# One encoder layer on one core: the convolution of a pair in two blocks, more first operands before the last norm, the last norm's steps together, the third block of output weights earlier

## The chip, the cores and the metric

The kernel runs on one core of a Trainium2 chip. The metric is the device time of one execution in microseconds (us); lower is better. A core has five engines that run their own instruction lists in order and wait for each other through semaphores: TensorE (PE in the profile), VectorE (DVE), ScalarE (ACT), GpSimd (POOL) and SyncE (SP, which here issues transfers). PE writes its sums to eight banks of PSUM; DVE and ACT read them from there. The projections keep fp32 accuracy with three matmuls over a high and a low part of each operand.

## The reference

One layer of an encoder over 1024 positions of width 1024. Only the second half matters for this change:

```
hn = rms_norm(x, norm1_g);  proj = hn @ w_in
out_a = global_gqa_attention(...);  out_b = dilated_mixture_attention(...)
mixed = concat([rms_norm(out_a, outa_norm_g), rms_norm(out_b, outb_norm_g)])
x = x + mixed @ w_out
h = rms_norm(x, norm2_g)
u = h @ w_up                                   # 1024 x 5632
u = conv(u, conv_w, width 3, per channel) + conv_b
x = x + (gelu(u[:, :2816]) * u[:, 2816:]) @ w_down
```

## The kernel before

**Stages.** The profiled execution shows them one after the other on PE: the first projection, mixer A (attention), mixer B (dilated windows), the output projection `mixed @ w_out` with the second norm (to about 683 us), the up projection with convolution and gate (683 to 1085 us), and the down projection (to the end at 1330 us).

**The output projection and the last norm.** It goes over eight row blocks i of 128 positions. `h2_a(i)` adds the residual on DVE (L929), takes the squares on ACT (L935), and forms the norm's factor in a chain of one-element operations on DVE and one square root on ACT (L936, L937, L938, the four steps of a Newton iteration at L191 to L194); L942 writes the normed rows `hn(i)`. `h2_b(i, half)` transposes these on PE (L180, four per half) and takes the result out of PSUM into the operands of the up projection: L204 and L957 to L965, with sums and differences of row blocks that the seven-product scheme below needs. `t_split` (L972 on ACT, L973 on DVE) splits such a sum into high and low part. The last two blocks are 6 and 7. PE does the first two products of the up projection while norm 7 is made, then the transposes of block 7.

**The up projection.** It takes the channels in 22 pairs j of two channel tiles (u = 0, 1). Even pairs hold gate channels, the odd pair behind them the matching value channels. A pair is computed by a fast scheme with seven products of half size instead of eight; `product` (L1247 to L1249) is twelve matmuls. The products of a pair come in the order n = 1, 6, 7, 5, 2, 4, 3. The seven results are put together by copies on ACT (n = 1 and 2, L1254 and L1264) and by adds on DVE (L1251, for n = 6, 7, 5, 4 and 3). Four PSUM banks serve the even pairs and four the odd ones. Within a pair n = 4 writes the bank of n = 7, and n = 3 that of n = 5, so PE can start n = 4 only when DVE has done the add of n = 7, and n = 3 only after the add of n = 5.

`wu_prep(m)` makes the first operand of a product some products ahead: sums of weight blocks on POOL (L1221, L1222, L1224, L1226), the high part on ACT (L1230), the low part on DVE, or on POOL for n = 2 and 4 (both L1231). `conv(j, u)` is the convolution of a channel tile: the middle tap with the bias on ACT (L1278, 1024 positions), then four side taps on DVE (L1280: two of 768 positions and two of 255). `gate(j, u)` is the gelu on ACT (L1284) and the product on DVE (L1285) for two pairs together, and `gate_sums` the sums that the down projection needs, on POOL (L1294, behind one-element operations L1299), with stores to a scratch in HBM.

**What sets the order.** The functions are called in a written order, and a scheduler fixes each engine's list from it before the run. Where the author wants an order that the data do not force, a copy of one element (a "tick") writes into a place that a later operation overwrites, after reading something that must be done first. In the loop over products, the convolutions of both tiles of pair j are called right behind its product n = 3, and, for an odd pair, the two gates behind them. On DVE that puts eight taps and two gate products in one run between the add of n = 3 and the adds of the next pair.

**Weights of the output projection.** `wo_load` and `wo_split` bring its eight blocks of weights in and split them (L869 on ACT, L874 on DVE), some during mixer A and some between the heads of mixer B.

Of the kernel before, what the change touches and what calls it, by code (L numbers as in the profile page):

```python
# [14 lines left out]
AF = mybir.ActivationFunctionType  # L15
# [4 lines left out]
D = 1024  # L20
# [83 lines left out]
R_T4 = R_W + 4096  # L104
R_OP = [R_W + 8192, R_W + 9216, R_K2A + 6144, R_K2A + 7168, R_K2A + 4096, R_K2A + 5120]
# [18 lines left out]
def tile_encoder_layer(ctx, tc, x, w_in, gains, outg, norm1_g, norm2_g, w_out, w_up, conv_w, conv_b,  # L124
# [84 lines left out]
    def qab(tt):  # L209
        return O_QAB + 1024 * tt  # L210
# [493 lines left out]
    def load_tmx(h):  # L704
        dma(f(F_TMX[h % 2], 1344), tmx[h])
# [181 lines left out]
    def mix_t(i):  # L887
        return SM_T + 16 * (i % 3)
# [36 lines left out]
    def h2_a(i):  # L925
        t = SM_T + 48 + 8 * (i % 2)
        o = qab(seq(i))
        for hf in range(2):
            vec.scalar_tensor_tensor(f(o + 512 * hf, 512), bank(pj(i, hf)), f(mix_t(i) + 6, 1),  # L929
                                     f(F_X + 1024 * (i % 2) + 512 * hf, 512), op0=OP.mult, op1=OP.add)  # L930
        if i < 6:
            act(f(hn(i), 1024), f(o, 1024), AF.Square, accum_out=f(t, 1))
        else:
            for hf in range(2):
                act(f(hn(i) + 512 * hf, 512), f(o + 512 * hf, 512), AF.Square, accum_out=f(t + 5 + hf, 1))  # L935
            vec.tensor_tensor(f(t, 1), f(t + 5, 1), f(t + 6, 1), op=OP.add)  # L936
        vec.tensor_scalar(f(t + 1, 1), f(t, 1), 1.0 / D, EPS, op0=OP.mult, op1=OP.add)  # L937
        act(f(t + 2, 1), f(t + 1, 1), AF.Sqrt)  # L938
        newton(f(t + 3, 1), f(t + 1, 1), f(t + 2, 1), f(t + 4, 1))
        n = 1024 if i < 6 else 512  # L940
        for k in range(0, 1024, n):
            vec.scalar_tensor_tensor(f(hn(i) + k, n), f(o + k, n), f(t + 3, 1), f(F_G2 + k, n), op0=OP.mult, op1=OP.mult)  # L942
        dma(rscr[seq(i)], f(o, 1024))
# [3 lines left out]
    def h2_b(i, half):  # L947
        b = next_tr()
        for k in range(4):
            tr_f(b, k, f(hn(i) + 512 * half + 128 * k, 128))  # L950
        pair, x0 = seq(i) % 4, xs(i)
        t1, t2, t3, t4 = [t_raw(n, pair) for n in (1, 2, 3, 4)]
        if seq(i) < 4:
            evac_split(x0 + 512 * half, b)
            act((t1, t4)[half], bank(b), AF.Copy)
        elif half == 0:
            act(t3, bank(b), AF.Copy)  # L957
            vec.tensor_tensor(t1, bank(b), t1, op=OP.subtract)
            act(r(x0, 512), t1, AF.Copy)
            (gp if i < 6 else vec).tensor_tensor(r(x0 + 1024, 512), t1, rf(x0, 512), op=OP.subtract)  # L960
        else:
            evac_split(x0 + 512, b)
            vec.tensor_tensor(t2, bank(b), t1, op=OP.subtract)
            vec.tensor_tensor(t3, bank(b), t3, op=OP.subtract)
            (gp if i < 6 else vec).tensor_tensor(t4, t4, t2, op=OP.subtract)  # L965

    def t_raw(n, i):
        return f((F_TA[i], qab(i + 4) + 512, qab(i + 4), F_TD[i])[n - 1], 512)

    def t_split(n, i, eng):  # L970
        o = (R_T2, R_T3, R_T4)[n - 2] + 1024 * i
        act(r(o, 512), t_raw(n, i), AF.Copy)  # L972
        eng.tensor_tensor(r(o + 512, 512), t_raw(n, i), rf(o, 512), op=OP.subtract)  # L973

# [139 lines left out]
    for g in range(16):  # L1114

        prep += a_prep(g + 1) if g < 15 else []
        if g == 14:
            prep += [lambda: b_split(0)] + b_prep(0)
        tail = a_main(g, prep, tail, late, {14: (1, 1, 1, 1, 1, 2, 2, 2), 15: (2, 2, 2, 2, 1, 1, 1, 1)}.get(
            g, (1, 1, 1, 1, 1, 1, 1, 0)),  # L1120
                      (0, 2, 2, 2, 1, 1, 1, 1))
        if g == 7:
            dma(f(F_CNT, 384), cnt)
            gp.memset(fp(F_VCN + 64, [66, 8]), 1.0)
            load_vc(0)
        if g in (4, 7):
            wo_load(g // 7)
        if g == 9:
            load_tmx(1)
# [143 lines left out]
    def conv(j, u):  # L1273
        c = tile_of(j, u)
        i = F_U[2 * (j % 2) + u]
        a = acc(j, u)
        w = [f(O_CW + 44 * t + c, 1) for t in range(4)]
        act(f(a, 1024), f(i, 1024), AF.Identity, scale=w[1], bias=w[3])  # L1278
        for w_, o, d, n in ((w[0], 256, 0, 768), (w[0], 1, 768, 255), (w[2], 0, 256, 768), (w[2], 768, 1, 255)):
            vec.scalar_tensor_tensor(f(a + o, n), f(i + d, n), w_, f(a + o, n), op0=OP.mult, op1=OP.add)  # L1280

    def gate(j, u):
        a, v = acc(j - 1, u), acc(j, u)
# [136 lines left out]
    for i in range(8):  # L1420
        if i < 7:
            proj_out(i + 1, 0, 0)
            mix_tr(i + 1, 1)
            proj_out(i + 1, 0, 1)
        if i == 6:
            wu_load(1)
            for m in range(4):
                wu_prep(m)
            for q in range(2):
                t_split(2, q, vec)  # L1430
        if 0 < i < 7:
# [12 lines left out]
        if i < 6:  # L1444
            x_load(i + 2)
# [6 lines left out]
    h2_b(7, 0)  # L1452
    h2_b(7, 1)
    t_split(2, 3, vec)
    for o in (F_S[0], F_S[2]):

        vec.tensor_copy(f(o, 1), f(mix_t(7) + 10, 1))
    wu_prep(4)
    for q in range(4):
        t_split(3, q, vec)  # L1460
    wu_prep(5)
    for q in range(4):
        t_split(4, q, vec)
    dealt = []
    for m in range(2, len(order)):
        j, n = order[m]
        product(m)
        wu_prep(m + 4)

        if n in (2, 4) or n == 3 and j % 2 == 0 or n == 1 and j % 2:  # L1470
            take(dealt, 1)
        if n == 3 and j < NPAIR - 1:
            conv(j, 0)
            conv(j, 1)
            if j % 2:
                gate(j, 0)
                gate(j, 1)
                dealt += gate_sums(j)
        if j == NPAIR - 1:
            if n == 5:  # L1480
                for q in range(4):
                    d_load(q)
            if n == 4:
                d_prep(0)
                d_load(4)
            if n == 3:
                d_prep(1)
                d_prep(2)
                d_load(5)
                d_load(6)  # L1490
    last = NPAIR - 1
    for m in range(len(steps)):
        n, q = steps[m]
        down(m)
        d_prep(m + 3)
        if m < 2:
            conv(last, m)
# [68 lines left out]
```

## Time and profile before

| | |
|---|---|
| median of three runs | 1331.51 us (1330.01 to 1332.91) |
| the profiled execution, its own time | 1332.38 us |
| its span | 1330.6 us |
| PE busy | 1301.8 us (98%) |
| DVE busy | 1013.6 us (76%) |
| ACT busy | 681.6 us (51%) |
| POOL busy | 387.0 us (29%) |

PE's busy time is near the span, so a gain can only come from the few places where PE stands or runs at a lower clock, and a loss from new ones. The shares of the other engines are means over the whole span; in the up projection DVE is far above its mean. An engine's idle time is printed with what ended it, in brackets: `[0.58 <-DVE bigf L1251]` means that the engine stood for 0.58 us and went on when DVE's instruction of line 1251 was done.

### The profile page before, as it was taken

How to read it: one execution, taken by the hardware profiler on the slowest of the kernel's cores; microseconds unless marked ns; L12 is line 12 of the kernel's file. 1: busy time of each engine (PE TensorE's matmuls, PEld its weight loads, DVE VectorE, ACT ScalarE, POOL GpSimd, SP SyncE). 2: the span in 40 equal slices, each digit the busy share in tenths (PEclk: the TensorE clock that was granted, in tenths of full speed). 3: DMA queues.
4: the chain of work that ended last, by engine and by line, in shares of the span. 5: the costliest groups of instructions: out<-in, count | busy, mean ns of one | idle time of the engine just before them, and what ended most of it. 6: DMA issues, size and time to landing. Idle time of an engine off the chain costs nothing.

```text
span 1330.6 us, 20124 instructions
## 1 busy us (share of the span) xinstructions
PE 1301.8 (98%) x7559; PEld 1130.2 (85%) x7559; DVE 1013.6 (76%) x1599; ACT 681.6 (51%) x1070; POOL 387.0 (29%) x304
## 2 busy tenths in 40 slices
PE   7999999999999999999999999999999999999998
PEld 7999999999999888878877888888888888888887
DVE  4987687556655777876588999999999999586664
ACT  7855564555545676674365344444444445244341
POOL 0611122000111222100115666556756653100000
PEclk9999999999999999999999999999999999999999
DMA  7145211001002454443122322322232325897873
GB/s 258 52 112 127 80 40 52 17 1 36 2 9 61 99 143 114 99 144 111 64 88 72 119 103 103 103 89 95 103 119 101 106 95 190 303 309 231 295 229 105
DMA packets 120500, 152.28 MB, mean 114 GB/s; under 512 B 50962, under 2 KB 77010, under 8 KB 119890
## 3 DMA queue, kind: packets, MB, share of 16 engines
q1 hardware_dynamic: 118609, 143.65, 33.4%
q0 software_dynamic: 1792, 7.34, 2.5%
q8 instruction: 59, 0.97, 0.3%
q14 instruction: 40, 0.32, 0.1%
HBM read 112.95 MB, written 33.82 MB: 110 GB/s over the span
## 4 chain that ended last, share of the span: by engine, by line
PE 79%; DVE 12%; ACT 4%; issue 4%; DMA 1%; SPq 0%; DVEq 0%; ACTq 0%
PE ps L659 8%; PE ps L1247 7%; PE ps L1248 7%; PE ps L1249 7%; PE ps L1380 5%; PE ps L1378 5%; PE ps L1379 5%; DVE bigf L1280 5%; PE ps L411 4%; PE ps L412 3%; PE ps L413 3%; PE ps L664 3%; PE ps L637 2%; PE ps L665 2%; PE ps L918 2%
## 5 line engine op out<-in xcount | busy, mean ns | idle before, releaser
L1247 PE MATMUL ps<-bigr 128*128 128x512 f32 x616 | 241.8, 393 | 6.2 <-DVE bigf L1251 5.6
L1248 PE MATMUL ps<-bigr 128*128 128x512 f32 x616 | 240.3, 390 | 0.0
L1249 PE MATMUL ps<-bigr 128*128 128x512 f32 x616 | 240.1, 390 | 0.0
L1280 DVE SCALAR_TENSOR_TENSOR bigf<-bigf 128x768 f32<-128x768 f32 (+1 forms) x176 | 178.5, 1073 | 26.4 <-ACT bigf L1278 26.3
L1230 ACT ACTIVATE bigr<-bigf 128x512 fp32r<-128x512 f32 x154 | 93.2, 625 | 139.4 <-POOL bigf L1222 70.3
L659 PEld LDWEIGHTS ps<-bigf 128*128 128x128 f32 x1024 | 139.6, 191 | 10.4
L1247 PEld LDWEIGHTS ps<-bigr 128*128 128x128 f32 x616 | 116.1, 188 | 34.9 <-DVE bigf L1251 9.0
L1358 ACT ACTIVATE bigr<-bigf 128x1024 fp32r<-128x1024 f32 x77 | 80.8, 1060 | 118.8 <-PE ps L1380 85.7
L1249 PEld LDWEIGHTS ps<-bigr 128*128 128x128 f32 x616 | 116.0, 188 | 24.4
L1248 PEld LDWEIGHTS ps<-bigr 128*128 128x128 f32 x616 | 116.1, 188 | 23.6
L659 PE MATMUL ps<-bigf 128*128 128x65 f32 x1024 | 135.0, 267 | 0.0
L411 PE MATMUL ps<-bigr 128*128 128x256 f32 x448 | 127.2, 284 | 1.2 <-ACT bigf L295 1.2
L1231 DVE TENSOR_TENSOR bigr<-bigf,bigr 128x512 fp32r<-128x512 f32 x112 | 125.2, 1135 | 3.2 <-ACT bigr L1230 2.6
L412 PE MATMUL ps<-bigr 128*128 128x256 f32 x448 | 126.8, 283 | 0.0
L413 PE MATMUL ps<-bigr 128*128 128x256 f32 x448 | 126.7, 283 | 0.0
L667 ACT ACTIVATE bigf<-ps 128x512 f32<-128x512 f32 x128 | 76.0, 597 | 93.5 <-PE ps L665 92.4
L1378 PE MATMUL ps<-bigr 128*128 128x512 f32 x308 | 119.8, 389 | 0.0
L1380 PE MATMUL ps<-bigr 128*128 128x512 f32 x308 | 119.8, 389 | 0.0
L1379 PE MATMUL ps<-bigr 128*128 128x512 f32 x308 | 119.8, 389 | 0.0
L1359 DVE TENSOR_TENSOR bigr<-bigf,bigr 128x1024 fp32r<-128x1024 f32 x77 | 93.0, 1222 | 26.0 <-ACT bigr L1358 25.0
L638 DVE TENSOR_REDUCE bigf<-ps 128x1 f32<-128x512 f32 x128 | 86.3, 690 | 23.5 <-PE ps L637 21.6
L411 PEld LDWEIGHTS ps<-bigr 128*128 128x128 f32 x448 | 85.8, 192 | 1.9 <-ACT bigf L295 1.6
(233 smaller groups left out, 2870.0 us busy)
## 6 DMA issues: line engine op xcount, KB each, us to landing
bigf<-w_down SPq DMA_DIRECT2D x99, 256.0 KB, 4.3
bigf<-w_up SPq DMA_DIRECT2D x44, 512.0 KB, 3.6
bigf<-gscr SPq DMA_DIRECT2D x77, 256.0 KB, 4.0
gscr<-bigf SPq DMA_DIRECT2D x33, 512.0 KB, 2.6
bigf<-w_in SPq DMA_DIRECT2D x8, 1024.0 KB, 5.1
bigf<-x SPq DMA_DIRECT2D x15, 512.0 KB, 7.0
bigf<-tmx SPq DMA_DIRECT2D x8, 672.0 KB, 5.5
bigf<-w_out SPq DMA_DIRECT2D x8, 512.0 KB, 4.8
```

The source lines that it names most:

```text
L411: mm(o, ah, wh, start=(k == 0 and t % 2 == 0 and n != 2), stop=False, skip_group_check=True)
L412: mm(o, ah, wl, start=False, stop=False, skip_group_check=True)
L413: mm(o, al, wh, start=False, stop=(k == 3), skip_group_check=True)
L659: mm(bank(ob, 65, 66 * i), f(slots[kt] + 128 * i, 128), f(F_VA + 132 * kt + 66 * kv, 65), start=(kt == 0 and i == 0), stop=(kt == 7), skip ...
L1231: (gp if n in (2, 4) and m > 3 else vec).tensor_tensor(rp(o + 512, [128, 4], [1, 128]), src, rfp(o, [128, 4], [1, 128]), op=OP.subtract)
L1247: mm(bank(b), wh, th, start=(k == 0 and n in (1, 5, 6, 7)), stop=False, skip_group_check=True)
L1248: mm(bank(b), wh, tl, start=False, stop=False, skip_group_check=True)
L1249: mm(bank(b), wl, th, start=False, stop=(k == 3), skip_group_check=True)
L1280: vec.scalar_tensor_tensor(f(a + o, n), f(i + d, n), w_, f(a + o, n), op0=OP.mult, op1=OP.add)
L1378: mm(o, ah, r(d, 512), start=(q == 0 and n in (1, 5, 2)), stop=False, skip_group_check=True)
L1379: mm(o, ah, r(d + 1024, 512), start=False, stop=False, skip_group_check=True)
L1380: mm(o, al, r(d, 512), start=False, stop=(q == NQ - 1), skip_group_check=True)
```

## The change

There are four parts.

1. **The last norms' steps together.** For blocks 6 and 7 the mean and the constant are added to the first half's sum as soon as it is there, and one operation joins the second half; one step leaves the chain. A tick that reads `hn(7)` (L958 of the new code) now stands in front of the evacuations of block 6, and such a tick (L980) in front of the splits of T3 and T4 for two of their four parts, so that on DVE all this comes behind norm 7. Two subtractions of block 6 go from DVE to POOL.
2. **Two more first operands ahead.** `wu_prep(4)` and `wu_prep(5)` are called before the last norm with the first four; the places of six operand buffers and two weight blocks move for it.
3. **The convolution in two blocks.** `conv` now returns two blocks per tile: the middle tap with the two taps of `w[0]`, and the two taps of `w[2]`. The loop does one block behind each of the products n = 1, 6, 7 and 5 of the next pair. The middle tap of u = 1 waits for a tick (L1290) that reads what the add of the next pair's n = 7 writes. The two gates come one each behind n = 2 and n = 4 of the even pair, the four steps of the gate sums behind n = 3 of the even pair and n = 1, 6 and 7 of the odd one. Twenty-one ticks are added.
4. **The third block of output weights.** Block 4 is loaded and split during mixer A, instead of loaded behind mixer A and split in the last head of mixer B; the other loads and splits move one place.

```diff
-F_WOR = [O_F + o for o in (4960, 4960, 2560, 3616, 6304, 4960, 2560, 6304)]
+F_WOR = [O_F + o for o in (4960, 4960, 2560, 3616, 3616, 4960, 6304, 2560)]
...
-            vec.tensor_tensor(f(t, 1), f(t + 5, 1), f(t + 6, 1), op=OP.add)
-        vec.tensor_scalar(f(t + 1, 1), f(t, 1), 1.0 / D, EPS, op0=OP.mult, op1=OP.add)
+                if hf == 0:
+                    vec.tensor_scalar(f(t, 1), f(t + 5, 1), 1.0 / D, EPS, op0=OP.mult, op1=OP.add)
+            vec.scalar_tensor_tensor(f(t + 1, 1), f(t + 6, 1), 1.0 / D, f(t, 1), op0=OP.mult, op1=OP.add)
...
+        if i == 6:
+            vec.tensor_copy((r(x0 + 1536, 1), f(qab(seq(6) % 4 + 4), 1))[half == 0], f(hn(7), 1))
...
+        if n > 2 and i < 2:
+            vec.tensor_copy(r(o, 1), f(hn(7), 1))
...
-    for k, (g0, kt) in enumerate(((6, 4), (8, 4))):
+    for k, g0, kt in ((0, 6, 4), (4, 7, 4), (1, 8, 4)):
...
-    wo_early = {(5, 0): [(wo_load, 2)], (6, 0): [(wo_load, 3), (wo_load, 4)], (7, 0): [(wo_load, 5)],
-                (7, 1): [(wo_split, 2), (wo_load, 6)], (7, 3): [(wo_split, 3)], (7, 5): [(wo_split, 4), (wo_load, 7)]}
+    wo_early = {(5, 0): [(wo_load, 2)], (6, 0): [(wo_load, 3), (wo_load, 6)], (7, 0): [(wo_load, 5)],
+                (7, 4): [(wo_split, 3)], (7, 5): [(wo_split, 2), (wo_load, 7)]}
...
-        act(f(a, 1024), f(i, 1024), AF.Identity, scale=w[1], bias=w[3])
-        for w_, o, d, n in ((w[0], 256, 0, 768), (w[0], 1, 768, 255), (w[2], 0, 256, 768), (w[2], 768, 1, 255)):
-            vec.scalar_tensor_tensor(f(a + o, n), f(i + d, n), w_, f(a + o, n), op0=OP.mult, op1=OP.add)
+        def mid():
+            if u and j < last:
+                vec.tensor_copy(f(a, 1), f(F_U[2 * ((j + 1) % 2) + 1], 1))
+            act(f(a, 1024), f(i, 1024), AF.Identity, scale=w[1], bias=w[3])
+
+        def side(w_, *spans):
+            for o, d, n in spans:
+                vec.scalar_tensor_tensor(f(a + o, n), f(i + d, n), w_, f(a + o, n), op0=OP.mult, op1=OP.add)
+
+        return [lambda: (mid(), side(w[0], (256, 0, 768), (1, 768, 255))),
+                lambda: side(w[2], (0, 256, 768), (768, 1, 255))]
...
-            for m in range(4):
+            for m in range(6):
                 wu_prep(m)
...
-        if n in (2, 4) or n == 3 and j % 2 == 0 or n == 1 and j % 2:
-            take(dealt, 1)
-        if n == 3 and j < NPAIR - 1:
-            conv(j, 0)
-            conv(j, 1)
+        if n == 3 and j < last:
+            taps += conv(j, 0) + conv(j, 1)
             if j % 2:
-                gate(j, 0)
-                gate(j, 1)
+                gates += [lambda j=j, u=u: gate(j, u) for u in range(2)]
                 dealt += gate_sums(j)
+        else:
+            take(taps, 1)
+        if j % 2 == 0 and n in (2, 4):
+            take(gates, 1)
+        if n == 3 and j % 2 == 0 or n in (1, 6, 7) and j % 2:
+            take([] if gates else dealt, 1)
```

What the scheduler makes of it is read from the engines' lists. In the new code the lines from the up projection on are higher: the matmuls L1247 to L1249 are L1255 to L1257, the low part L1231 is L1239, the add L1251 is L1259, the taps L1280 are L1295, the gate L1285 is L1303, the gate sums L1294 and L1299 are L1312 and L1317, and the norm's last write L942 is L945.

DVE around the last norm. Before, from L937 to the write of `hn(7)`:

```order
L937 TENSOR_SCALAR bigf<-bigf 128x1
L960 TENSOR_TENSOR bigr<-bigf,bigr 128x512
L964 TENSOR_TENSOR bigf<-ps,bigf 128x512
L191 RECIPROCAL bigf<-bigf 128x1
L965 TENSOR_TENSOR bigf<-bigf 128x512
L192 TENSOR_TENSOR bigf<-bigf 128x1
L973 TENSOR_TENSOR bigr<-bigf,bigr 128x512
L193 SCALAR_TENSOR_TENSOR bigf<-bigf 128x1
L1231 TENSOR_TENSOR bigr<-bigf,bigr 128x512
L194 SCALAR_TENSOR_TENSOR bigf<-bigf 128x1
L973 TENSOR_TENSOR bigr<-bigf,bigr 128x512
L942 SCALAR_TENSOR_TENSOR bigf<-bigf 128x512 x2
```

The same place in the new code:

```order
L937 TENSOR_SCALAR bigf<-bigf 128x1
L929 SCALAR_TENSOR_TENSOR bigf<-ps,bigf 128x512
L938 SCALAR_TENSOR_TENSOR bigf<-bigf 128x1
L191 RECIPROCAL bigf<-bigf 128x1
L192 TENSOR_TENSOR bigf<-bigf 128x1
L193 SCALAR_TENSOR_TENSOR bigf<-bigf 128x1
L194 SCALAR_TENSOR_TENSOR bigf<-bigf 128x1
L945 SCALAR_TENSOR_TENSOR bigf<-bigf 128x512 x2
L958 COPY bigf<-bigf 128x1
L958 CAST bigr<-bigf 128x1
L980 CAST bigr<-bigf 128x1 x2
L204 TENSOR_TENSOR bigr<-ps,bigr 128x512
```

The six operations of 512 elements that stood between the norm's small steps are gone from there; block 6's evacuations (from L204 on) follow the norm. On PE the first four transposes of block 7 stand eight matmuls earlier than before and the second four stand four matmuls earlier.

DVE in the up projection, from the add of an odd pair's n = 3 to the adds of the even pair behind it. Before:

```order
L1251 TENSOR_TENSOR bigf<-ps,bigf 128x512
L1280 SCALAR_TENSOR_TENSOR bigf<-bigf 128x768
L1251 TENSOR_TENSOR bigf<-ps,bigf 128x512
L1280 SCALAR_TENSOR_TENSOR bigf<-bigf 128x255 x2
L1280 SCALAR_TENSOR_TENSOR bigf<-bigf 128x768 x2
L1280 SCALAR_TENSOR_TENSOR bigf<-bigf 128x255 x2
L1280 SCALAR_TENSOR_TENSOR bigf<-bigf 128x768
L1285 TENSOR_TENSOR bigf<-bigf 128x1024 x2
L1251 TENSOR_TENSOR bigf<-ps,bigf 128x512
L1231 TENSOR_TENSOR bigr<-bigf,bigr 128x512
```

The same place in the new code, to the first taps of u = 1:

```order
L1259 TENSOR_TENSOR bigf<-ps,bigf 128x512 x2
L1295 SCALAR_TENSOR_TENSOR bigf<-bigf 128x768
L1295 SCALAR_TENSOR_TENSOR bigf<-bigf 128x255 x2
L1295 SCALAR_TENSOR_TENSOR bigf<-bigf 128x768
L1239 TENSOR_TENSOR bigr<-bigf,bigr 128x512
L1303 TENSOR_TENSOR bigf<-bigf 128x1024
L1259 TENSOR_TENSOR bigf<-ps,bigf 128x512
L1239 TENSOR_TENSOR bigr<-bigf,bigr 128x512
L1259 TENSOR_TENSOR bigf<-ps,bigf 128x512
L1239 TENSOR_TENSOR bigr<-bigf,bigr 128x512
L1290 COPY bigf<-bigf 128x1
L1295 SCALAR_TENSOR_TENSOR bigf<-bigf 128x768
```

Four taps have gone from the first run to behind the add of n = 7 and the tick, with the middle tap of u = 1 on ACT between tick and taps; behind these follow the 255 tap, the add of n = 5, the other two taps of u = 1, one low part, the second gate and one more low part. The odd pair behind has the same list without the gates.

POOL from the gates' end on. Before:

```order
L1222 TENSOR_TENSOR bigf<-bigf 128x512
L1299 TENSOR_TENSOR bigf<-bigf 128x1
L1294 TENSOR_TENSOR bigf<-bigf 128x512 x3
L1226 TENSOR_TENSOR bigf<-bigf 128x512
L1299 TENSOR_TENSOR bigf<-bigf 128x1
L1294 TENSOR_TENSOR bigf<-bigf 128x512
L1224 TENSOR_TENSOR bigf<-bigf 128x512
```

In the new code (L1229, L1230, L1232 and L1234 are the weight sums L1221, L1222, L1224 and L1226):

```order
L1312 TENSOR_TENSOR bigf<-bigf 128x512
L1317 TENSOR_TENSOR bigf<-bigf 128x1
L1312 TENSOR_TENSOR bigf<-bigf 128x512
L1239 TENSOR_TENSOR bigr<-bigf,bigr 128x512
L1312 TENSOR_TENSOR bigf<-bigf 128x512 x2
L1229 TENSOR_TENSOR bigf<-bigf 128x512
L1239 TENSOR_TENSOR bigr<-bigf,bigr 128x512
L1230 TENSOR_TENSOR bigf<-bigf 128x512
L1234 TENSOR_TENSOR bigf<-bigf 128x512
```

The gate sums stood behind the weight sum L1222 of a pair; now they stand ahead of the sums L1229 and L1230 (before, L1221 and L1222), in the stretch in which DVE has the taps of the even pair's u = 0.

More of the change, by code (lines that the diff above doesn't have):

```diff
@@ L98 @@
 F_JK3 = O_F + 7840
-F_WOR = [O_F + o for o in (4960, 4960, 2560, 3616, 6304, 4960, 2560, 6304)]
+F_WOR = [O_F + o for o in (4960, 4960, 2560, 3616, 3616, 4960, 6304, 2560)]
 R_T2 = R_W
 R_T3 = R_K2A
-R_T4 = R_W + 4096
-R_OP = [R_W + 8192, R_W + 9216, R_K2A + 6144, R_K2A + 7168, R_K2A + 4096, R_K2A + 5120]
+R_T4 = R_K2A + 4096
+R_OP = [R_W + 4096 + 1024 * i for i in (4, 5, 2, 3, 0, 1)]
 F_UR = [O_F + 5632, O_F + 6656, O_F + 7680, O_F + 2560]
@@ L935, in h2_a @@
                 act(f(hn(i) + 512 * hf, 512), f(o + 512 * hf, 512), AF.Square, accum_out=f(t + 5 + hf, 1))
[L936 to L937 removed]
+                if hf == 0:
+                    vec.tensor_scalar(f(t, 1), f(t + 5, 1), 1.0 / D, EPS, op0=OP.mult, op1=OP.add)
+            vec.scalar_tensor_tensor(f(t + 1, 1), f(t + 6, 1), 1.0 / D, f(t, 1), op0=OP.mult, op1=OP.add)
+        if i < 6:
+            vec.tensor_scalar(f(t + 1, 1), f(t, 1), 1.0 / D, EPS, op0=OP.mult, op1=OP.add)
         act(f(t + 2, 1), f(t + 1, 1), AF.Sqrt)
@@ L1125, in tile_encoder_layer @@
             load_vc(0)
[L1126 to L1129, printed above, removed]
+        if g in (4, 5, 7):
+            wo_load({4: 0, 5: 4, 7: 1}[g])
+        if g in (9, 10):
+            load_tmx(10 - g)
         if g == 11:
@@ L1426, in tile_encoder_layer @@
             wu_load(1)
-            for m in range(4):
+            for o in (F_S[0], F_S[2]):
+                vec.tensor_copy(f(o, 1), f(mix_t(7) + 10, 1))
+            for m in range(6):
                 wu_prep(m)
@@ L1454, in tile_encoder_layer @@
     t_split(2, 3, vec)
-    for o in (F_S[0], F_S[2]):
-        vec.tensor_copy(f(o, 1), f(mix_t(7) + 10, 1))
-    wu_prep(4)
     for q in range(4):
         t_split(3, q, vec)
-    wu_prep(5)
     for q in range(4):
         t_split(4, q, vec)
-    dealt = []
+    last = NPAIR - 1
+    taps, gates, dealt = [], [], []
     for m in range(2, len(order)):
@@ L1468, in tile_encoder_layer @@
         wu_prep(m + 4)
-        if n in (2, 4) or n == 3 and j % 2 == 0 or n == 1 and j % 2:
-            take(dealt, 1)
-        if n == 3 and j < NPAIR - 1:
-            conv(j, 0)
-            conv(j, 1)
+        if n == 3 and j < last:
+            assert not taps
+            taps += conv(j, 0) + conv(j, 1)
             if j % 2:
-                gate(j, 0)
-                gate(j, 1)
+                gates += [lambda j=j, u=u: gate(j, u) for u in range(2)]
                 dealt += gate_sums(j)
+        else:
[4 more added lines that the diff above has]
+            take([] if gates else dealt, 1)
         if j == NPAIR - 1:
@@ L1496, in tile_encoder_layer @@
         if m < 2:
-            conv(last, m)
+            take(conv(last, m), 2)
         if m == 2:
```

8 lines of the change are left out of this document (3 added, 5 removed).

## The prediction

> **What bounds the kernel now.** I read the page first, then who waits for whom on PE, then the timelines around the longest of these waits.
>
> ```profile
> PE 1301.8 (98%) x7559; PEld 1130.2 (85%) x7559; DVE 1013.6 (76%) x1599; ACT 681.6 (51%) x1070; POOL 387.0 (29%) x304
> ```
>
> ```profile
> PE ps L1247 <- DVE bigf L1251: 5.6, 10, 0.6
> PE ps L180 <- DVE bigf L942: 2.1, 1, 2.1
> PE ps L793 <- DVE bigr L822: 1.4, 1, 1.4
> PE ps L1247 <- ACT bigr L972: 0.5, 1, 0.5
> ```
>
> PE is the bound, and the change aims at three of its waits: ten for the adds in the up projection, one for the last norm (with one for a split behind it), one in mixer B. The timeline of PE shows what each costs.
>
> ```profile
> 690.30 0.39 PE L1247 MATMUL ps<-bigr 128*128 128x512 f32 x1
> 690.52 0.39 PE L1248 MATMUL ps<-bigr 128*128 128x512 f32 x1
> 692.98 0.66 PE L180 MATMUL ps<-bigf 128*128 128x128 f32 x4 [2.07 <-DVE bigf L942]
> ...
> 694.13 0.78 PE L1247 MATMUL ps<-bigr 128*128 128x512 f32 x1
> ...
> 697.58 0.40 PE L1249 MATMUL ps<-bigr 128*128 128x512 f32 x1
> ```
>
> ```profile
> 877.17 0.39 PE L1248 MATMUL ps<-bigr 128*128 128x512 f32 x1
> 877.40 0.39 PE L1249 MATMUL ps<-bigr 128*128 128x512 f32 x1
> 878.37 0.50 PE L1247 MATMUL ps<-bigr 128*128 128x512 f32 x1 [0.58 <-DVE bigf L1251]
> 878.70 0.39 PE L1248 MATMUL ps<-bigr 128*128 128x512 f32 x1
> ```
>
> Undisturbed matmuls start 0.2275 us apart, so a product of twelve takes 2.73, a pair 19.1 and two pairs 38.2. At the norm PE loses 692.98 - 690.52 - 0.23 = 2.23. From 694.13 eight matmuls take 3.45 instead of 1.82, another 1.63, and there the clock is halved:
>
> ```profile
> 694.00:697.30 3.30, 3.30 (x11) 2.62 (x10) 2.94 (x6) 2.42 (x5) 1.28 (x1) 0.50 0.00 0
> ```
>
> With the 0.5 for L972 and some 0.3 of slow restarts the last norm costs 4.7. One up-projection wait costs 0.74 and 0.10 in the next interval, so 0.26 more than the idle time printed; ten cost 5.6 + 10 x 0.26 = 8.2. They come once per two pairs, always in the odd pair.
>
> The next view groups DVE's work by form over one such period, from one wait to the next.
>
> ```profile
> L1231 DVE TENSOR_TENSOR bigr<-bigf,bigr 128x512 fp32r<-128x512 f32 x11 | 13.1, 1207 | 0.2 <-ACT bigr L1230 0.2
> L1280 DVE SCALAR_TENSOR_TENSOR bigf<-bigf 128x768 f32<-128x768 f32 x8 | 10.9, 1379 | 2.6 <-ACT bigf L1278 2.6
> L1251 DVE TENSOR_TENSOR bigf<-ps,bigf 128x512 f32<-128x512 f32 x10 | 6.8, 680 | 0.0
> L1280 DVE SCALAR_TENSOR_TENSOR bigf<-bigf 128x255 f32<-128x255 f32 x8 | 6.4, 843 | 0.0
> L1285 DVE TENSOR_TENSOR bigf<-bigf 128x1024 f32<-128x1024 f32 x2 | 2.4, 1214 | 0.0
> ```
>
> ```profile
> 838.40:877.40 39.00, 38.38 (x170) 31.45 (x168) 36.21 (x39) 17.26 (x25) 25.26 (x18) 1.00 0.29 101
> ```
>
> DVE is busy 36.21 of 39.00 us and stands 2.6 of the rest behind two middle taps: here it has no time left either. Much of its time is contention with POOL. Minimum, median and maximum of each line over the up projection:
>
> ```profile
> L1280 DVE SCALAR_TENSOR_TENSOR bigf<-bigf x146: 470/1006/2057, 719.7 to 1078.4; 128x768 f32<-128x768 f32 x74, 128x255 f32<-128x255 f32 x72
> L1251 DVE TENSOR_TENSOR bigf<-ps,bigf x95: 674/678/693, 720.6 to 1079.5; 128x512 f32<-128x512 f32 x95
> L1231 DVE TENSOR_TENSOR bigr<-bigf,bigr x94: 674/1178/1827, 721.2 to 1075.7; 128x512 fp32r<-128x512 f32 x94
> L1285 DVE TENSOR_TENSOR bigf<-bigf x18: 1208/1214/1220, 735.1 to 1048.1; 128x1024 f32<-128x1024 f32 x18
> ```
>
> ```profile
> 867.96 3.48 DVE L1280 SCALAR_TENSOR_TENSOR bigf<-bigf 128x255 f32<-128x255 f32 x2
> 869.40 4.01 DVE L1280 SCALAR_TENSOR_TENSOR bigf<-bigf 128x768 f32<-128x768 f32 x2
> ```
>
> ```profile
> 866.53 0.68 DVE L1251 TENSOR_TENSOR bigf<-ps,bigf 128x512 f32<-128x512 f32 x1
> 867.13 0.90 DVE L1280 SCALAR_TENSOR_TENSOR bigf<-bigf 128x255 f32<-128x255 f32 x1
> ```
>
> ```profile
> 869.15 3.44 POOL L1231 TENSOR_TENSOR bigr<-bigf,bigr 128x512 fp32r<-128x512 f32 x2
> 875.87 1.29 POOL L1222 TENSOR_TENSOR bigf<-bigf 128x512 f32<-128x512 f32 x1 [3.28 <-DVE bigr L1231]
> ```
>
> ```profile
> L1230 ACT ACTIVATE bigr<-bigf 128x512 fp32r<-128x512 f32 x154 | 93.2, 625 | 139.4 <-POOL bigf L1222 70.3
> ```
>
> While POOL has work they take turns, one instruction each: a 768 tap takes 1.00 alone and 2.05 in turn, a 255 tap 0.47 and about 1.5, a low part L1231 0.68 and 1.7 to 1.8. The adds read PSUM and stay at 0.68. Instructions overlap by 0.08 (867.13 starts before 866.53 + 0.68), so in a row each counts 0.08 less. Alone the period's taps and low parts would take 8 x 1.00 + 8 x 0.47 + 11 x 0.68 = 19.2 instead of 30.4: contention is 11.2.
>
> **The change, part by part.**
>
> *Convolution in two blocks.* No tap is removed. Before, the middle tap of u = 1 ran beside the taps of u = 0, so DVE waited for one middle tap per pair:
>
> ```profile
> 864.90 1.70 DVE L1280 SCALAR_TENSOR_TENSOR bigf<-bigf 128x768 f32<-128x768 f32 x1 [1.31 <-ACT bigf L1278]
> ```
>
> Now the tick, the middle tap and the tap of u = 1 stand directly behind each other, so DVE waits 1.31 twice per pair. That adds 2.6 us per two pairs to an engine that had none, and the ticks 0.2 (one-element operations take 0.15 in the norm's rows below). The adds of n = 7 do come before most taps now, so the old wait at n = 4 goes. What is late next is the add of n = 5 of the odd pair, which PE's n = 3 needs. I walk DVE's new list in order, with the prices above less 0.08.
>
> From an odd pair's n = 3 add to the next even pair's: five adds 3.0; two middle taps 2.8; tick 0.1; u = 0's taps behind POOL's two low parts 1.8 + 1.4 + 0.4 + 0.9 = 4.5; u = 1's alone 2.65; two gates 2.3; five low parts, three alone (1.8) and two behind POOL sums that the gates held up (1.0 and 1.7), 4.5. Together 19.9, and some five separate waits, 0.1: 20.0. PE needs 7 x 2.73 = 19.1, so this add is 0.9 late.
>
> From there to the end of the odd pair's n = 5 add, with POOL's low parts, gate sums and weight sum beside it: add 0.6; middle tap 1.4; taps 0.9 + 1.4 + 1.4 + 2.0 = 5.7; low part 1.7; add 0.6; low part 1.1; add of n = 7 0.7; then the last low part, which needs POOL's sum L1230 and ACT's high part (the 0.63 of L1230), and POOL reaches that sum only behind the gate sums: a wait of 1.2; low part 0.6; tick 0.15; middle tap 1.3; two taps 1.3; add 0.7; waits 0.1. Together 17.15.
>
> DVE needs 37.15 from the one to the other. PE has the thirteen products between, 35.5, and 0.3 more goes for its last matmul's own length and both hand-overs: PE stands 37.15 + 0.3 - 35.5 = 1.95, with the restart 2.05 per two pairs where it lost 0.84. The bounds: contention in this walk is 8.2 instead of 11.2; none relieved gives 5, relieved to 6 nothing.
>
> The first odd pair has no gates beside it: 0. The second I put at half, 1.1, the next eight at 2.05, the last, whose neighbours differ, at 1.1 (0 to 2). Sum 18.6 against 8.2: **+10.4**. The preparation of the down projection is DVE work behind the last taps: +0.5 (0 to 1.5).
>
> *The last norm and the first operands.* DVE before:
>
> ```profile
> 683.39 0.74 DVE L929 SCALAR_TENSOR_TENSOR bigf<-ps,bigf 128x512 f32<-128x512 f32 x1
> ...
> 686.58 0.15 DVE L936 TENSOR_TENSOR bigf<-bigf 128x1 f32<-128x1 f32 x1
> ...
> 688.50 0.15 DVE L191 RECIPROCAL bigf<-bigf 128x1 f32<-128x1 f32 x1
> ...
> 690.50 0.15 DVE L194 SCALAR_TENSOR_TENSOR bigf<-bigf 128x1 f32<-128x1 f32 x1
> ...
> 691.18 2.41 DVE L942 SCALAR_TENSOR_TENSOR bigf<-bigf 128x512 f32<-128x512 f32 x2
> ```
>
> The small steps take 0.15 each and 4.6 us in all, since six operations of 512 stand between. Back to back: last residual 684.13, square and root on ACT about 0.7, five steps 0.8, two writes 1.4: done near 687.2 instead of 693.6. PE comes to its transposes eight matmuls earlier, 690.74 - 1.82 = 688.9. But block 6's evacuations are behind the norm now, and free their bank near 689.2: a wait of 0.3, and about 0.5 behind it for the second transposes and the splits. The low parts of the two operands made ahead leave the stretch behind the norm, but the splits of T3 and T4 now stand there, and run on to n = 3 of pair 0, whose bank I expect 1.2 late. Together 2.0 (0.8 to 3.5) for 4.7: **-2.7**. Of this, 1.6 is the half clock. [...] In the trace the half clock lasts 3.4 us and follows this gap, while the gaps of 0.6 have none.
>
> *Third block of weights.* Mixer B's 1.4 at L793 is made a little shorter, since one split leaves that head: -0.2 (0 to -0.5). The split in mixer A lies beside other work of ACT and DVE, and PE waits there for neither; without that cover it would cost about 1.
>
> Sum: 10.4 + 0.5 - 2.7 - 0.2 = +8.0. The profiled execution took 1332.38, which gives 1340.4; the median of the runs shown is 0.9 lower, 1331.51, which gives 1339.5.
>
> **The rivals.**
>
> (a) Not slower: gate and POOL do not hold each other up. The trace never shows a gate beside POOL: L1285 is 1208 to 1220 throughout. In the new list a POOL sum meets each gate. The nearest row is L1231, the same operation at half the length, which is held. If gates are not, the two low parts behind them cost 0.6 each instead of 1.0 and 1.7, the even half 18.5 and its add on time, so the 0.9 goes and PE stands 1.15 per two pairs: 1.15 x 8 + 1.2 for the two half ones - 8.2 + 0.5 - 2.9 = -0.2, so 1331.3. It decides there: below 0.84 + 2.4/8.5 = 1.1 per two pairs the kernel isn't slower. [...]
>
> (b) The middle taps' gaps take up so much of POOL's work that contention falls to 6 and PE never waits in the steady pairs: 1331.5 - 8.2 + 1.5 - 2.4 = 1322.4. Against it: POOL has 18 operations per period (the row of 838.40) and the gaps hold four.
>
> (c) The new wait of nearly 2 us halves the clock, as the one of 2.07 did. Where that falls on n = 3, on which DVE waits in turn, it costs up to 1.6 each, otherwise PE's spare time hides it: 8 x 1.6 gives 1352 at most.
>
> (d) The last norm gains nothing, since its evacuations now wait instead: 1342.2.
>
> **How the numbers follow.** The forecast, with (d) in it, has 0.74, (c) 0.10, (a) 0.11, (b) 0.05. 1339.5 is the forecast's. The range runs from 1331, where (a) ends, to 1346 (contention 0.8 per period above the walk's, or (c) in half of the periods); the forecast alone has 1335 to 1344. A difference below 0.2%, 2.7 us, can't be told from none. (a) is mostly within it, with 0.02 faster: faster 0.07, same 0.09, slower 0.84.
>
> **What would show it.** In the new profile: PE's wait for the add of about 1.8 us once per two pairs, now at n = 3 of the odd pair; DVE idle about 1.3 before taps four times in 40 us; DVE's taps of u = 1 at 1.00 and 0.47; POOL sums beside the gates of over 2 us; the wait at L180 for the norm below 0.5 and no half clock there. Wrong would be the forecast if low parts behind the gates take 0.68, or if the period of two pairs is below 39.2.

## The result, and the profile after

The changed kernel takes 1348.29 us (median of four runs, 1346.60 to 1348.97) against 1332.21 us (1330.01 to 1333.32) in the same comparison: 1.0122 times the time before, interval 1.0106 to 1.0138. The forecast was slower, by 8 us and to 1346 at the most; it is slower by 16.

Who waits for whom on PE (us in total, times, longest):

```profile
PE ps L1255 <- DVE bigf L1259: 14.3, 10, 1.9
PE ps L793 <- DVE bigr L822: 1.5, 1, 1.5
PE ps L180 <- DVE bigf L964: 1.2, 1, 1.2
PE ps L1397 <- DVE bigr L1377: 1.2, 1, 1.2
...
PE ps L1396 <- ACT bigr L1376: 0.9, 1, 0.9
...
PE ps L180 <- DVE bigf L945: 0.2, 1, 0.2
```

The waits for the adds in the up projection have gone from 5.6 to 14.3 us. PE's wait before the transposes of block 7 has gone from 2.1 us (for the norm's write L942) to 1.2 (for L964, an evacuation of block 6); the 0.2 for L945 is a new wait, for norm 6, before the transposes of block 6. Two more new waits stand in the down projection. How far the changed kernel lags at the same matmul of the two traces shows where the time went:

| stretch | lag at its end, us | gained in it |
|---|---|---|
| first projection and before (to 210 us) | 0.73 | +0.73 |
| mixers and output projection | 0.94 | +0.2 |
| last norm, to the end of pair 0 | 0.14 | -0.8 |
| up projection | 12.5 | +12.4 |
| down projection | 16.6 | +4.1 |

In the first row no engine computes anything else than before; only a load, issued at 195.5 us, has moved, and 0.58 of the 0.73 is there at 100 us already. This is what single executions differ by. The lag at the end of the up projection is seen in the timeline of PE, before and after:

```profile
1116.73 0.39 PE L1249 MATMUL ps<-bigr 128*128 128x512 f32 x1
1116.96 0.39 PE L1378 MATMUL ps<-bigr 128*128 128x512 f32 x1
```

```profile
1129.27 0.39 PE L1257 MATMUL ps<-bigr 128*128 128x512 f32 x1
1129.49 0.39 PE L1396 MATMUL ps<-bigr 128*128 128x512 f32 x1
```

**The up projection.** One of the new waits, in PE's timeline:

```profile
842.50 0.39 PE L1257 MATMUL ps<-bigr 128*128 128x512 f32 x1
844.75 0.51 PE L1255 MATMUL ps<-bigr 128*128 128x512 f32 x1 [1.86 <-DVE bigf L1259]
845.09 0.60 PE L1256 MATMUL ps<-bigr 128*128 128x512 f32 x1
```

It costs 2.02 and 0.11 in the next interval, and the matmul behind it takes 0.60 instead of 0.39: the clock has fallen (0.50 from 845.10 to 848.52).

DVE's work by form over one period of two pairs (802.28 to 842.50, from wait to wait), and the busy time of the engines in it; the second row of the latter is the 3.4 us behind the wait at 844.75:

```profile
L1295 DVE SCALAR_TENSOR_TENSOR bigf<-bigf 128x768 f32<-128x768 f32 x8 | 10.8, 1352 | 5.3 <-ACT bigf L1291 5.3
L1239 DVE TENSOR_TENSOR bigr<-bigf,bigr 128x512 fp32r<-128x512 f32 x10 | 8.8, 893 | 1.2 <-ACT bigr L1238 1.2
L1295 DVE SCALAR_TENSOR_TENSOR bigf<-bigf 128x255 f32<-128x255 f32 x8 | 6.8, 864 | 0.0
```

```profile
802.28:842.50 40.22, 38.38 (x170) 31.45 (x168) 33.55 (x40) 17.21 (x25) 27.53 (x19) 1.00 0.29 98
845.20:848.60 3.40, 3.40 (x10) 2.63 (x9) 2.62 (x5) 1.58 (x2) 1.90 (x2) 0.51 0.00 0
```

DVE is busy for less than before (33.55 against 36.21 us), since contention has fallen: the taps and low parts take 26.4 us where they would take 18.6 alone, so 7.8 instead of 11.2 (10.4, when a low part of 1.46 us that lies across the edge of the older window is not counted). But it stands 5.3 us behind middle taps instead of 2.6, and 1.2 behind a high part. The period grows from 39.00 to 40.22.

The adds of n = 4 and n = 3 of the odd pair and of the even pair on DVE (806.90 and 825.83), the low part behind the second gate (825.23), and the odd half behind them, with the waits for the two middle taps and for the high part (840.61):

```profile
806.90 1.36 DVE L1259 TENSOR_TENSOR bigf<-ps,bigf 128x512 f32<-128x512 f32 x2
...
825.23 0.69 DVE L1239 TENSOR_TENSOR bigr<-bigf,bigr 128x512 fp32r<-128x512 f32 x1
825.83 1.47 DVE L1259 TENSOR_TENSOR bigf<-ps,bigf 128x512 f32<-128x512 f32 x2
828.66 6.69 DVE L1295 SCALAR_TENSOR_TENSOR bigf<-bigf 128x768 f32<-128x768 f32 x4 [1.36 <-ACT bigf L1291]
835.27 1.78 DVE L1239 TENSOR_TENSOR bigr<-bigf,bigr 128x512 fp32r<-128x512 f32 x1
...
838.69 0.68 DVE L1259 TENSOR_TENSOR bigf<-ps,bigf 128x512 f32<-128x512 f32 x1
840.61 0.69 DVE L1239 TENSOR_TENSOR bigr<-bigf,bigr 128x512 fp32r<-128x512 f32 x1 [1.25 <-ACT bigr L1238]
...
842.68 1.02 DVE L1295 SCALAR_TENSOR_TENSOR bigf<-bigf 128x768 f32<-128x768 f32 x1 [1.31 <-ACT bigf L1291]
```

POOL beside it and beside the two gates (which DVE starts at 814.75 and 824.09, 1.21 and 1.22 long):

```profile
814.97 2.14 POOL L1230 TENSOR_TENSOR bigf<-bigf 128x512 f32<-128x512 f32 x1 [2.35 <-DVE bigr L1239]
...
824.26 2.81 POOL L1232 TENSOR_TENSOR bigf<-bigf 128x512 f32<-128x512 f32 x1 [2.95 <-DVE bigr L1239]
...
831.64 2.90 POOL L1312 TENSOR_TENSOR bigf<-bigf 128x512 f32<-128x512 f32 x2
...
838.18 1.74 POOL L1230 TENSOR_TENSOR bigf<-bigf 128x512 f32<-128x512 f32 x1
```

POOL's sum at the first gate starts 0.22 us behind the gate and takes 2.14, where such a sum alone takes 1.29 (818.94): it ends at 817.11, 1.15 us after the gate's end at 815.96, while the gate takes 1.21 as before. So here the gate, which started first, was not held up, and the sum was, by 0.85. The sum at the second gate takes 2.81: it ends at 827.07, 1.15 us after the end, at 825.92, of the low part behind that gate, and the low part takes 0.69 as if alone. In the odd half POOL has no pause from 827 to 840, and its last sum (838.18) ends at 839.92, 0.55 us after DVE's add of n = 7 (838.69 + 0.68). Only then does ACT make the high part that the last low part waits for (839.95, 0.63 long).

**The last norm** on DVE:

```profile
684.23 0.74 DVE L929 SCALAR_TENSOR_TENSOR bigf<-ps,bigf 128x512 f32<-128x512 f32 x1
685.77 0.15 DVE L937 TENSOR_SCALAR bigf<-bigf 128x1 f32<-128x1 f32 x1 [0.79 <-ACT bigf L935]
685.84 0.74 DVE L929 SCALAR_TENSOR_TENSOR bigf<-ps,bigf 128x512 f32<-128x512 f32 x1
...
688.73 1.41 DVE L945 SCALAR_TENSOR_TENSOR bigf<-bigf 128x512 f32<-128x512 f32 x2
```

The steps are together, but the second residual add (685.84) now stands behind L937, which waits 0.79 us for the square of the first half. `hn(7)` is done at 690.1 instead of 687.2 as forecast (before: 693.6); 0.9 of the difference is the lag that this trace has here already.

**The down projection.** ACT around the last up product, before and after, then the first loads of `w_down` that are issued behind the last stores of the gate sums, before and after:

```profile
1115.61 1.24 ACT L1278 ACTIVATE bigf<-bigf 128x1024 f32<-128x1024 f32 x1
```

```profile
1128.98 1.06 ACT L1302 ACTIVATE bigf<-bigf 128x1024 f32<-128x1024 f32 x1 [2.71 <-DVE bigf L1295]
1129.95 1.04 ACT L1376 ACTIVATE bigr<-bigf 128x1024 fp32r<-128x1024 f32 x1
1130.90 1.23 ACT L1291 ACTIVATE bigf<-bigf 128x1024 f32<-128x1024 f32 x1
```

```profile
1136.14 0.32 SPq L1317 DMA_DIRECT2D gscr<-bigf  x1
1136.55 0.38 SPq L1335 DMA_DIRECT2D bigf<-w_down  x1
```

```profile
1151.42 0.32 SPq L1335 DMA_DIRECT2D gscr<-bigf  x1
1151.83 0.38 SPq L1353 DMA_DIRECT2D bigf<-w_down  x1
```

Counted from the first matmul of the down projection (1116.96 and 1129.49), the last pair's first middle tap starts at -1.35 before and +1.41 now: on ACT it stands behind the gelu L1302, which waited 2.71 us for dealt taps of the pair ahead. So the last gates, their sums and the stores come 2.75 us later (19.2 to 21.9), and the loads queued behind the stores too, of `w_down` and of the sums from the scratch. ACT's high part waits for such a load of the scratch, PE for the operands made from it, 0.9 and 1.2 us, and the clock falls behind it (0.50 from 1159.13 to 1162.54):

```profile
1156.64 1.06 ACT L1376 ACTIVATE bigr<-bigf 128x1024 fp32r<-128x1024 f32 x1 [12.46 <-DMA bigf<-gscr]
1157.75 0.49 PE L1396 MATMUL ps<-bigr 128*128 128x512 f32 x1 [0.90 <-ACT bigr L1376]
1159.43 0.80 PE L1397 MATMUL ps<-bigr 128*128 128x512 f32 x1 [1.18 <-DVE bigr L1377]
```

### The profile page after: what moved, and what is told of

Same layout as the page of the kernel before. It is cut to its first block, busy times and chain, and to the rows that moved or that the text cites. A ratio compares the mean times of both kernels' runs of the same rounds, so it can differ in the third digit from the quotient of the medians.

```text
span 1347.2 us, 20157 instructions
## 1 busy us (share of the span) xinstructions
PE 1307.9 (97%) x7559; PEld 1133.2 (84%) x7559; DVE 986.2 (73%) x1626; ACT 681.9 (51%) x1070; POOL 403.8 (30%) x306
## 4 chain that ended last, share of the span: by engine, by line
PE 60%; DVE 17%; issue 7%; ACT 6%; POOL 6%; DMA 2%; SPq 0%; POOLq 0%; ACTq 0%; DVEq 0%
PE ps L659 8%; DVE bigf L1295 5%; PE ps L1397 5%; PE ps L1398 5%; PE ps L1396 5%; PE ps L1255 3%; PE ps L1257 3%; PE ps L1256 3%; POOL bigf L1312 3%; PE ps L664 3%; PE ps L637 2%; DVE bigr L1239 2%; PE ps L665 2%; ACT bigf L1291 2%; PE ps L841 2%
## 5 line engine op out<-in xcount | busy, mean ns | idle before, releaser
L1255 PE MATMUL ps<-bigr 128*128 128x512 f32 x616 | 243.0, 395 | 14.6 <-DVE bigf L1259 14.3
L1257 PE MATMUL ps<-bigr 128*128 128x512 f32 x616 | 241.7, 393 | 0.0
L1295 DVE SCALAR_TENSOR_TENSOR bigf<-bigf 128x255 f32<-128x255 f32 (+1 forms) x176 | 174.0, 1039 | 53.1 <-ACT bigf L1291 53.1
L1255 PEld LDWEIGHTS ps<-bigr 128*128 128x128 f32 x616 | 116.7, 190 | 43.7 <-DVE bigf L1259 18.8
L659 PEld LDWEIGHTS ps<-bigf 128*128 128x128 f32 x1024 | 139.8, 191 | 10.4
L1257 PEld LDWEIGHTS ps<-bigr 128*128 128x128 f32 x616 | 116.7, 190 | 24.6
L1397 PE MATMUL ps<-bigr 128*128 128x512 f32 x308 | 120.6, 392 | 1.2 <-DVE bigr L1377 1.2
L1396 PE MATMUL ps<-bigr 128*128 128x512 f32 x308 | 120.4, 391 | 0.9 <-ACT bigr L1376 0.9
L1239 DVE TENSOR_TENSOR bigr<-bigf,bigr 128x512 fp32r<-128x512 f32 x112 | 102.5, 925 | 8.4 <-ACT bigr L1238 8.4
```

The lines of the kernel that those rows point to most:

```text
L659: mm(bank(ob, 65, 66 * i), f(slots[kt] + 128 * i, 128), f(F_VA + 132 * kt + 66 * kv, 65), start=(kt == 0 and i == 0), stop=(kt == 7), skip ...
L1239: (gp if n in (2, 4) and m > 3 else vec).tensor_tensor(rp(o + 512, [128, 4], [1, 128]), src, rfp(o, [128, 4], [1, 128]), op=OP.subtract)
L1255: mm(bank(b), wh, th, start=(k == 0 and n in (1, 5, 6, 7)), stop=False, skip_group_check=True)
L1257: mm(bank(b), wl, th, start=False, stop=(k == 3), skip_group_check=True)
L1396: mm(o, ah, r(d, 512), start=(q == 0 and n in (1, 5, 2)), stop=False, skip_group_check=True)
L1397: mm(o, ah, r(d + 1024, 512), start=False, stop=False, skip_group_check=True)
```

## The experiments

Theory 1: the loss is made by part 3, since the tick puts the middle tap of u = 1 between two instructions of DVE, which has no time to spare. Rivals: the parts spoil each other; the dealt gates and POOL's sums are the cause without the tick. Times of before in the first four: 1331.71 us, in the last four 1331.43 us.

**Part 3 alone.** The kernel before with the new `conv` and the new loop over products:

```diff
-            conv(j, 0)
-            conv(j, 1)
+            taps += conv(j, 0) + conv(j, 1)
...
+        else:
+            take(taps, 1)
```

> The kernel before with part 3 alone (the convolution in two blocks, gates and gate sums dealt). Theory 1, that part 3 makes all of the loss: ten waits of PE for the adds with about 14 us of idle time, most of 1.9 at n = 3 of the odd pair, a halved clock behind some of them, and about 4 us at the start of the down projection; 1347 to 1350 us. The last norm costs what it did, 2.1 us at L180. Theory 2, that the parts spoil each other (fewer operands ready, other buffers): below 1342 us.

Measured: 1347.05 us, ratio 1.0109 (1.0092 to 1.0126). PE's waits:

```profile
PE ps L1247 <- DVE bigf L1251: 13.7, 10, 1.9
...
PE ps L180 <- DVE bigf L942: 2.0, 1, 2.0
...
PE ps L1387 <- ACT bigr L1367: 1.2, 1, 1.2
PE ps L1388 <- DVE bigr L1368: 0.8, 1, 0.8
```

As theory 1 expected: both the waits of the up projection and those at the start of the down projection come with part 3, and nothing else is needed for them.

**Parts 1, 2 and 4 alone.** The changed kernel with the old `conv` and the old loop:

```diff
-            taps += conv(j, 0) + conv(j, 1)
+            conv(j, 0)
+            conv(j, 1)
...
-        else:
-            take(taps, 1)
```

> The changed kernel with the convolution, gates and gate sums as before (parts 1, 2 and 4 alone). Theory 1: the up projection's ten waits are the old 5.6 us, the wait at L180 for L964 stays at 1.2 us with no halved clock behind it, and the time is 0 to 2 us below before, 1330 to 1332.5 us. Theory 2: above 1335 us.

Measured: 1331.17 us, ratio 0.9994 (0.9985 to 1.0004): no difference that can be told, where the prediction had 2.9 us for these parts. The waits at L180 are the changed kernel's (1.2 for L964, 0.2 for L945), and no half clock follows them (the mean clock of the span is 1.000). Of the eleven waits for the adds ten are the old ones, and one of 0.9 is that of pair 0, which the changed kernel has too:

```profile
PE ps L1255 <- DVE bigf L1259: 6.7, 11, 0.9
```

**Without the tick.**

```diff
-            if u and j < last:
-                vec.tensor_copy(f(a, 1), f(F_U[2 * ((j + 1) % 2) + 1], 1))
```

> The changed kernel without the tick in front of the middle tap of u = 1; dealing of taps, gates and gate sums as in the change. Theory 1, that two more middle taps are exposed on DVE by the tick: DVE waits for a middle tap about 1.3 us per pair as before instead of 2.6, PE's waits fall to below 0.7 us each, no halved clock, the start of the down projection has no wait again; 1328 to 1332 us. Theory 2, that the dealt gates and POOL's sums are the cause: waits near 2 us stay, 1343 us or more.

Measured: 1326.99 us, ratio 0.9962 (0.9947 to 0.9976), faster than before and than theory 1 expected. PE's waits for the adds, and then DVE's for the middle taps, without the tick and in the changed kernel:

```profile
PE ps L1255 <- DVE bigf L1259: 1.8, 3, 1.0
```

```profile
DVE bigf L1295 <- ACT bigf L1291: 26.3, 20, 1.3
```

```profile
DVE bigf L1295 <- ACT bigf L1291: 53.1, 40, 1.6
```

Twenty-one instructions of 0.15 us, whose own time is 3 us, decide about 21 us. Without them the middle tap of u = 1 runs beside the taps of u = 0, as it did before. No wait is left at L1396 and L1397. Too short for the list of waits, 0.4 us per period is still lost at n = 3 of the odd pair (0.3 at 874.99 and 0.1 behind it), some 3 us in all.

**The old steps of the mean.**

```diff
-                if hf == 0:
-                    vec.tensor_scalar(f(t, 1), f(t + 5, 1), 1.0 / D, EPS, op0=OP.mult, op1=OP.add)
-            vec.scalar_tensor_tensor(f(t + 1, 1), f(t + 6, 1), 1.0 / D, f(t, 1), op0=OP.mult, op1=OP.add)
+            vec.tensor_tensor(f(t, 1), f(t + 5, 1), f(t + 6, 1), op=OP.add)
+        vec.tensor_scalar(f(t + 1, 1), f(t, 1), 1.0 / D, EPS, op0=OP.mult, op1=OP.add)
```

> The changed kernel with the old steps of the mean for blocks 6 and 7 (both halves' sums added, then the constant), so that both residual adds L929 of block 7 stand together on DVE. Theory 1, that the step on the first half holds the second residual add behind a wait of 0.8 us: the write of hn(7) ends about 1 us earlier, the wait of 1.2 us at L180 falls to 0.2 to 0.4, the time is about 1 us below the changed kernel, near 1347. Theory 2, that block 6's evacuations on DVE are the limit: the wait at L180 stays above 0.9 us.

Measured: 1346.28 us, ratio 1.0107 (1.0092 to 1.0122); the interval overlaps that of the changed kernel, so the microsecond is read from the trace. Both residual adds stand together, and the wait before the transposes of block 7 is 0.3 (for L961, the L964 of the changed kernel) instead of 1.2; the 0.3 for L942 is the wait for norm 6:

```profile
681.75 1.40 DVE L929 SCALAR_TENSOR_TENSOR bigf<-ps,bigf 128x512 f32<-128x512 f32 x2
683.94 0.16 DVE L936 TENSOR_TENSOR bigf<-bigf 128x1 f32<-128x1 f32 x1 [0.79 <-ACT bigf L935]
```

```profile
PE ps L180 <- DVE bigf L942: 0.3, 1, 0.3
PE ps L180 <- DVE bigf L961: 0.3, 1, 0.3
```

So the shortened chain was longer by about the 0.8 that its early step waits: against the write of norm 6, `hn(7)` is done 0.9 us earlier here than in the changed kernel.

**The tick kept, POOL's sums later.**

```diff
-        if n == 3 and j % 2 == 0 or n in (1, 6, 7) and j % 2:
+        if n == 3 and j % 2 == 0 or n in (1, 2, 4) and j % 2:
             take([] if gates else dealt, 1)
```

> The changed kernel with the gate sums dealt later (behind n = 3 of the even pair and n = 1, 2 and 4 of the odd pair instead of n = 1, 6 and 7), the tick kept. Theory 1, that the tick's exposed middle taps alone are enough: PE's waits at n = 3 of the odd pair stay above 1.4 us, 1342 to 1347 us. Theory 2, that POOL's sums beside the taps of the odd half are enough by themselves: waits below 0.5 us, under 1332 us.

Measured: 1343.35 us, ratio 1.0091 (1.0078 to 1.0105), eight waits of 1.5 to 1.6:

```profile
PE ps L1255 <- DVE bigf L1259: 14.3, 11, 1.6
```

In this run DVE waits for a high part only once in the up projection, 0.5 us. So the wait of 1.2 behind POOL's late sum, which stands at the end of the odd half in the changed kernel, isn't needed for waits of that size.

**The tick kept, POOL's sums left out.**

```diff
-        t = lambda d, a, b, op: gp.tensor_tensor(f(d, 512), f(a, 512), f(b, 512), op=op)
+        t = lambda d, a, b, op: None
```

> The changed kernel with POOL's arithmetic of the gate sums left out (four sums per two pairs; the stores and the down projection work on what is in the buffers), tick kept. Theory 1 in its stronger form, the exposed middle taps whatever POOL does: waits above 1 us stay, 1338 us or more. Theory 3, that it takes both, the middle taps' two gaps of 1.3 us and about 3 us or more of contention with the four sums per two pairs: PE's waits in the steady pairs are gone (below 0.3), 1322 to 1329 us.

Measured: 1322.57 us, ratio 0.9935 (0.9917 to 0.9953). DVE still waits for the forty middle taps, 53.1 us as in the changed kernel, and PE for one add only:

```profile
PE ps L1255 <- DVE bigf L1259: 1.0, 1, 1.0
```

So theory 1 in its strict form falls. The exposed middle taps cost PE nothing where DVE has time for them; it takes both, the 2.6 us that they add per period and the contention with POOL's four sums. With the tick, moving the sums gains 5 us (waits of 1.5 to 1.6 instead of 1.9, and no half clock behind them, the clock being 1.00 from 800 to 1080 us), leaving them out gains 26.

At the start of the down projection it takes both too. Without POOL's sums ACT has the last pair's middle tap behind the gelu as in the changed kernel, but the gelu waits 1.30 us instead of 2.71, the middle tap starts at -1.37 from the first matmul of the down projection (before: -1.35), and PE has no wait there. The last pair's own sums are missing here as well, so the stores behind them can't be compared.

**Gates dealt, sums late, convolution at once.** With parts 1, 2 and 4:

```diff
             conv(j, 0)
             conv(j, 1)
             if j % 2:
-                gate(j, 0)
-                gate(j, 1)
+                gates += [lambda j=j, u=u: gate(j, u) for u in range(2)]
                 dealt += gate_sums(j)
+        if j % 2 == 0 and n in (2, 4):
+            take(gates, 1)
+        if n == 3 and j % 2 == 0 or n in (1, 2, 4) and j % 2:
+            take([] if gates else dealt, 1)
```

> Parts 1, 2 and 4 of the change, the convolution at once as before, the two gates dealt behind n = 2 and 4 of the even pair, the gate sums dealt later (n = 3 of the even pair, n = 1, 2 and 4 of the odd one). If DVE's run of eight taps and two gates, with POOL's sums beside the odd pair's, was what made the ten waits of before: no wait above 0.3 us in the steady pairs, 1322 to 1326 us. If the taps alone make them: ten waits of 0.5 us, 1330 us.

Measured: 1323.21 us, ratio 0.9942 (0.9929 to 0.9956). The ten waits are gone; two are left, both ahead of the steady pairs, of which the longer is that of pair 0:

```profile
PE ps L1255 <- DVE bigf L1259: 1.4, 2, 1.0
```

**The same with the old steps of the mean.** The last two diffs of these parts together.

> The kernel with the convolution at once, gates dealt and gate sums late, and the old steps of the mean for blocks 6 and 7. Theory 1: about 1 us below the same kernel with the new steps, 1321 to 1325 us; the wait at L180 is 0.2 to 0.6. Theory 2: the wait at L180 moves to the next products and the time is the same.

Measured: 1322.39 us (1321.56 to 1324.14), ratio 0.9936 (0.9923 to 0.9950), 9 us below before and 26 below the changed kernel. The 0.8 us to the run above is within the scatter; in the trace the two waits at L180 are 0.3 each, as expected.

## Why the prediction was right and wrong

- **The wait moves to n = 3 of the odd pair, 1.95 us and 0.1 behind it:** right in place and size, the size in part by luck. Six of the eight steady waits cost 2.0 and 0.1. The contention was put at 8.2 per period and is 7.8. The walk's two halves were each off by 0.9, in opposite directions, so that their sum, 37.1, is the forecast's 37.15. The n = 3 add of the even pair is not late (from the n = 3 add of one pair, 807.5, to that of the next, 826.6, it is 19.1, not 20.0): the low part behind the second gate was priced at 1.7, in turn with POOL, and takes 0.69, while POOL's sum ends 1.15 behind it. The odd half takes 18.1 instead of 17.15, since the first of its four taps contends with POOL as well (1.87, where the same tap of u = 1 takes 1.02).
- **The sum over the pairs, 18.6, is 20.6:** pair 3 1.2, six waits of 2.13, two of 0.9, and three stretches at half clock of 1.6 each. The step that failed is the exclusion of the half clock from the likeliest case: rival (c) with 0.10. It occurred behind three of the eight, and the two of 0.9 are those that follow such a stretch by a period, 1.2 shorter than the rest: the three cost 2.4 net. The last pair, put at 1.1, had no wait.
- **The preparation of the down projection, +0.5 (0 to 1.5), is +4.1:** the largest miss. The step looked at DVE's work behind the last taps. What counts is ACT, where the last pair's middle tap got behind a gelu that waited 2.71 us for dealt taps, and the transfer queue, where the next operands' loads are behind the stores of the last gate sums. PE's waits of 0.9 and 1.2 are 2.5 us of lost time with the restarts, and the half clock behind them takes 1.55.
- **The last norm, -2.7, is -0.8:** the old cost of 4.7 and the end of the half clock were right (the clock is 1.00 from 690 to 700 us). The step that failed is "last residual 684.13": the add had been taken from the old order, and in the new one, which the second list of the change shows, it stands behind L937 and its wait of 0.79, and ends at 686.6. The experiment with the old steps gives 0.9 us of this back. So block 6's evacuations free their bank later, and PE waits for them 1.2 instead of 0.3, which is in part what rival (d) says. The new wait for norm 6 costs another 0.5 that the sum did not have. The wait for pair 0's n = 3, put at 1.2, is 1.1.
- **The third block of weights, -0.2:** the wait at L793 is 1.5 instead of 1.4. No gain; two matmuls of the output projection moved from one side of the wait to the other.
- **Rival (a)** is refuted as a mechanism by the row of POOL's L1230 beside the gate (2.14 instead of 1.29), but half of its sign came: the low part behind the second gate takes 0.69, and the even pair's add is on time, as (a) had it. PE's wait did not fall to 1.15 only because the odd half was longer. Rival (b) is refuted by the waits. The range ended 2.3 us too low, because the misses of the down projection (3.6), the norm (1.9) and the up projection (2.0) all had the same sign.

What stays open is whether the tick alone, with the gates and sums of before, would have cost as much; no run shows it.

## What to carry to other kernels

An order that a one-element copy enforces can put another engine's instruction between two of a saturated engine: look on that engine's list for what each new wait stands ahead of, and price the gaps before the instructions. To relieve an engine, first take away what collides with it: here it was enough to deal two gates and to move four sums of POOL, and no tap had to be moved (which of the two does how much, no run separates). Walk also the end of such a stage, where the dealt work of the last pair meets the loads of the next stage in the same queue.

## What the hardware showed unexpectedly

The clock fell behind some waits of the same length and not behind others. In the changed kernel the trace has the clock at 0.50 in four stretches of 3.41 us, from 845.10, 927.02, 1087.45 and 1159.13 us, and the kernel before in one, from 694.01 (the first 16 and the last two us of each span aside). PE's six longest gaps in the up projection are 1.84 to 1.87 long. The half clock begins 0.35, 1.40 and 0.50 us after the end of those from 842.89, 923.77 and 1085.09 (1.86, 1.85 and 1.86 long); no half clock follows those from 802.67, 1004.60 and 1044.84 (1.84, 1.86 and 1.87). Nor is a single gap of that length needed: the fourth stretch comes with gaps of 0.90 and 1.18 at the start of the down projection. In the run with POOL's sums later, where the longest of these waits is 1.6, the clock is 1.00 from 800 to 1080 us.

The four starts lie 81.92, 160.43 and 71.68 us apart, which is 24.0, 47.0 and 21.0 times 3.413. An estimate from these starts alone: on a grid of 3.413 us through them, each of the three gaps that were followed lies between two points, and each of the three that were not has a point in it. Why that is so, and from which length on a gap is followed, no run shows. Behind each of the three PE lost 1.6 us more.
